# Moving the weighting with k–q products behind the substitution, in a two-layer hybrid encoder

## The chip, the cores and the metric

The kernel runs on one core of a Trainium2 chip. The metric is the device time of one execution in microseconds; the number compared is the median over several runs.

## The reference

The model has two residual layers over 256 tokens of 1024 channels. In each layer the normalised input is projected once into eleven segments. One branch is a bidirectional gated delta rule (8 heads, width 128), the other a differential softmax attention. Both are gated, projected, merged and projected out; a last RMSNorm closes. What the change touches is the delta rule:

```python
qkv = silu(short_conv(concat([q, k, v]), conv_w))     # 5 taps
q, k = l2norm(heads(q)), l2norm(heads(k))
decay = where(lower, exp(g_i - g_j), 0)                # g = cumulated log decays
L  = where(strict, (k*beta) @ k.T * decay, 0)
T  = inverse(eye + L)                                  # triangular solve
u, w = T @ (v*beta), T @ (k*beta*exp(g))
qk = where(lower, q @ k.T * decay, 0)
# per chunk: v_new = u - w @ state
#            o     = q*exp(g) @ state + qk @ v_new
#            state = state*exp(g_last) + (k*exp(g_last - g)).T @ v_new
```

It runs forwards and backwards, and the two outputs are added.

## The kernel before, in words

**Chunks and directions.** The kernel uses two chunks (`c`) of 128 tokens instead of the reference's 64, and keeps both directions (`d`) side by side. Heads are handled in two groups (`g`) of four.

**Projections.** Each is a stream over four pairs of weight rows (`kp`). A pair of 128 x 1024 elements is loaded (`raw`, L226, from SyncE's queue), cast to a high part (`hi`, L230, ScalarE) and reduced to a low part (`lo`, L232, VectorE: `raw − hi`). TensorE then does three matmuls per tile: hi with hi, lo with hi, hi with lo (L244–L246 token-major, L298–L302 feature-major). There are three buffers for `raw` and two each for `hi` and `lo`.

**Convolutions.** `conv` evacuates a feature-major projection of q, k or v: five taps on VectorE (L523 on ScalarE, L527 on VectorE), a tanh, a product, a transposition, and squares on ScalarE (L556). Group 1 of q (`conv("q", C_QA, 1, 1)`) is the last one ahead of the substitution.

**Decays.** `decays(g, c)` broadcasts the decay rows from DRAM into `B` (L618, issued from GpSimd's queue), lets GpSimd add to `kds` (L621) and mask (L624), and lets ScalarE take eight exponentials (L628). `weigh_k(g, c)` adds both directions (`dsum`, L634), forms the products of k with k on TensorE (`gram`, L611) and multiplies the two into `A` (L635). `weigh_q(g, c)` forms the products of k with q and multiplies them into `B` (L639, 128 x 1024 elements).

**Substitution.** `turn_blocks` exponentiates `kds` and stores the diagonal 32 x 32 blocks of `A` to DRAM and loads them back in another layout (L654–L657, GpSimd's queue). `take_blocks` copies them (L664), held behind the last q convolution. `substitute(0, 31)` does 62 VectorE operations (L670, L671), each depending on the one before it. `spread_blocks` copies and stores the result to `udr` (L674, L678).

**Merges and chunks.** `merges(g)` loads the blocks back (T64 at L705, U at L709) and joins them on TensorE (`y64p` at L723, `zt`, `z`, `y128p`, `zt128`). `chunks(g)` runs the recurrence; its second step scales k by the decays on GpSimd (L795, `ktm<-ktm,kds`, four products of 128 x 512 a layer) and its last step reads `B` (L821).

**Order.** A scheduler orders each engine's instructions by their place in the program and by a simulated time; attention heads (`head`), projections and the delta rule are interleaved in that way. `behind(ins)`, which is `tc.issue_after(ins)`, adds that what is traced in its block is queued behind `ins` on `ins`'s engine; `mark` holds such instructions. `bank_c` are two PSUM banks that the grams share with the convolutions' transpositions and the merges.

Of the kernel before, what the change touches and what calls it, by code (L numbers as in the profile page):

```python
# [12 lines left out]
ALU = mybir.AluOpType  # L13
# [4 lines left out]
P = 128  # L18
# [31 lines left out]
def hybrid_encoder(  # L50
# [47 lines left out]
    def last(ap, n):  # L98
        return ap.unsqueeze(ap.ndim).to_broadcast(list(ap.shape) + [n])
# [104 lines left out]
    def behind(ins):  # L204
        return nullcontext() if ins is None else tc.issue_after(ins)

    def weights(w, c0, n, nm, homes=(None,) * 4, ahead=True, later=None, spare=(), held=None):

        for kp in range(4):
            act, dve = (later or {}).get(kp, (None, None))
            with tc.high_priority(offset=HP) if ahead and homes[kp] is None else nullcontext():
                if homes[kp] is not None:
                    hi, lo = homes[kp][:, 0], homes[kp][:, 1]
                else:
                    hi = wpool.tile([P, 2, 512], F32R, tag="hi", name=f"hi_{nm}{kp}", bufs=2)
                    lo = wpool.tile([P, 2, 512], F32R, tag="lo", name=f"lo_{nm}{kp}", bufs=2)
                if kp in spare:  # L220
                    raw = work.tile([P, 2, 512], F32, tag="w4a", name=f"raw_{nm}{kp}", bufs=2)
                else:
                    raw = wpool.tile([P, 2, 512], F32, tag="raw", name=f"raw_{nm}{kp}", bufs=3)
                load = (held or {}).get(kp)
                with behind(load):
                    (nc.scalar if load else nc.sync).dma_start(  # L226
                        out=raw[:, :, :n],
                        in_=w[kp * 256 : (kp + 1) * 256, c0 : c0 + n].rearrange("(k p) c -> p k c", p=P))
                with behind(act):
                    high = S.copy(hi[:, :, :n], raw[:, :, :n]).ins  # L230
                with behind(dve):
                    mark[nm, kp] = high, V.tensor_tensor(lo[:, :, :n], raw[:, :, :n],  # L232
                                                         hi[:, :, :n].bitcast(F32), ALU.subtract).ins
            for k in range(2):
                yield 2 * kp + k, hi[:, k, :n], lo[:, k, :n]

    def proj_tm(act, w, c0, n, evac, nm, places=(None,) * 4, spare=(), later=None):

        accs = banks2(f"pp_{nm}")
        for kt, hi, lo in weights(w, c0, n, nm, places, later=later, spare=spare):  # L240
            for m in range(NM):
                ts_ = slice(m * P, (m + 1) * P)
                o = accs[m][:, :n]
                T.matmul(o, act[kt // 4][:, 0, kt % 4, ts_], hi, start=kt == 0, stop=False)  # L244
                T.matmul(o, act[kt // 4][:, 0, kt % 4, ts_], lo, start=False, stop=False)  # L245
                mark["proj"] = T.matmul(o, act[kt // 4][:, 1, kt % 4, ts_], hi, start=False,  # L246
                                        stop=kt == KT - 1).ins
                mark["done", kt] = mark["proj"]
        for m in range(NM):
            evac(m, accs[m][:, :n])  # L250
# [33 lines left out]
            evac(m, o)  # L284
            yield

    def proj_fm(act, w, c0, evac, nm):


        accs = [a.rearrange("p (b t) -> p b t", b=2) for a in banks2(f"pf_{nm}")]  # L290
        for kt, hi, lo in weights(w, c0, 512, nm, later=mark.pop("later", None)):
# [49 lines left out]
    for l in range(DEPTH):  # L341
# [98 lines left out]
        def qk_part(s_, i):  # L440
                def evac_qk(m, ps):
# [11 lines left out]
                    for b in range(4):  # L453
# [62 lines left out]
        def conv(seg, c_base, slot, g):  # L516
            def evac_conv(acc, b0):
# [86 lines left out]
        B = big.tile([P, NM, NH, 2, P], F32, tag="B", name=f"B{l}")  # L604
        kds = small.tile([P, 2, NH], F32, tag="kds", name=f"kds{l}")

        def gram(nm, g, c, slot):
            gp = bank_c(f"{nm}{l}{g}{c}")
            for j4 in range(4):
                kqh = kq[:, 4 * g + j4, c]  # L610
                T.matmul(gp[:, j4 * P : (j4 + 1) * P], kqh[:, 0, :], kqh[:, slot, :],  # L611
                         start=True, stop=True)
            return heads4(gp)

        def decays(g, c):
            hs4 = slice(4 * g, 4 * g + 4)
            dec = B[:, c, hs4].rearrange("p h d i -> p d h i")
            G.dma_start(out=B[:, c, hs4].rearrange("p h d i -> p (h d i)"),  # L618
                        in_=gdr[c, hs4].rearrange("h d i -> (h d i)").partition_broadcast(P))
            end = (P - 1) * (1 - c)  # L620
            G.tensor_tensor(kds[:, c, hs4], dec[:, c, :, end], lnc[:, c, c, hs4], ALU.add)  # L621
            for d in range(2):
                sg = 1 - 2 * d
                G.affine_select(out=dec[:, d], in_=dec[:, d], compare_op=ALU.is_ge, fill=BIG,  # L624
                                base=0, pattern=[[0, 4], [sg, P]], channel_multiplier=-sg)
                for j4 in range(4):
                    h = 4 * g + j4
                    S.activation(dec[:, d, j4, :], dec[:, d, j4, :], AF.Exp,  # L628
                                 bias=lnc[:, d, c, h : h + 1])

        def weigh_k(g, c):
            dec = B[:, c, 4 * g : 4 * g + 4].rearrange("p h d i -> p d h i")
# [1 line left out]
            V.tensor_tensor(dsum, dec[:, 0], dec[:, 1], ALU.add)  # L634
            V.tensor_tensor(A[:, g, c], gram("kk", g, c, 0), dsum, ALU.mult)  # L635

        def weigh_q(g, c):
            bv = B[:, c, 4 * g : 4 * g + 4]
            V.tensor_tensor(bv, gram("kq", g, c, 1).unsqueeze(2).to_broadcast([P, 4, 2, P]), bv, ALU.mult)  # L639


        osb = lambda g, c: kq[:, 4 * g : 4 * g + 4, c, 1, :]
# [28 lines left out]
                V.tensor_tensor(X[:, :nr, j + 1 :], X[:, :nr, j + 1 :], tv, ALU.subtract)  # L671

        def spread_blocks():
            V.tensor_copy(lt, X.rearrange("p c i -> p i c"))  # L674
            for d in range(2):
                ps_ = slice(64 * d, 64 * d + 64)
                for w, src_ in enumerate((X, lt) if d == 0 else (lt, X)):
                    G.dma_start(out=udr[w, :, :, 8 * d : 8 * d + 8].rearrange("b g t j i -> (b g) (t j i)"),  # L678
                                in_=src_[ps_].rearrange("p j i -> p (j i)"))


        tix = lambda d, c, j4: (2 * d + c) * 4 + j4
# [92 lines left out]
        def chunks(g):  # L775
# [16 lines left out]
                S.copy(flat(y1[d]), ps)  # L792
            yield
            for d in range(2):
                G.tensor_tensor(st[d], st[d], last(kds[:, d, hs4], P), ALU.mult)  # L795
# [282 lines left out]
```

## Time and profile before

| | |
|---|---|
| median of 3 runs | 779.93 us (778.48 to 781.05) |
| span of the profiled execution (first to last instruction) | 777.1 us |
| its launch time | not listed; the nearest figures are the runs above |
| TensorE (PE) busy | 758.2 us, 98% |
| VectorE (DVE) busy | 557.3 us, 72% |
| ScalarE (ACT) busy | 474.9 us, 61% |
| GpSimd (POOL) busy | 101.9 us, 13% |
| granted TensorE clock | 0.996 |

The engines run side by side, so the busy times add up to far more than the span. Matmuls are pipelined: two of them overlap in the trace, so a busy TensorE isn't necessarily at its peak. In lines of groups and waits, `a<-b` is what is written and what is read; `<-ENGINE tile Lnn` is what ended the idle time before.

### The profile page before, as it was taken

What the parts mean: (1) busy time and instruction counts of PE and PEld (TensorE: products, weight loads), DVE (VectorE), ACT (ScalarE), POOL (GpSimd) and SP (SyncE); (2) the same over time, 40 slices, a digit from 0 to 9 for tenths busy, and PEclk for the clock granted to TensorE, in tenths of its full rate; (3) what the DMA queues carried; (4) which work ended last, traced back from release to release, by engine and by line L of the source; (5) the groups of instructions that cost most, each with busy time, mean ns of one, the idle gap of its engine ahead of it and who ended that gap; (6) DMA issues with size and microseconds to landing.
All of it is one profiled execution on the core that took longest, in us unless ns stands there. A gap on an engine that the chain in (4) does not pass through costs nothing.

```text
span 777.1 us, 13805 instructions
## 1 busy us (share of the span) xinstructions
PE 758.2 (98%) x5222; PEld 647.7 (83%) x5222; DVE 557.3 (72%) x1051; ACT 474.9 (61%) x1042; POOL 101.9 (13%) x137
## 2 busy tenths in 40 slices
PE   8999999999999999999999999999999999999996
PEld 4899879887778888887889888899777788888784
DVE  5686878999974635377677776989999553536782
ACT  5657776557677744564554668655577776356551
POOL 5100461100030100010010025510001110001000
PEclk9999999999999999999999999999999999999998
DMA  7752756554496644346664256755446954343631
GB/s 227 240 177 78 224 146 198 174 172 136 112 207 187 210 135 129 117 144 210 215 224 136 82 160 221 194 170 161 141 137 174 233 164 160 114 133 111 213 110 54
DMA packets 77745, 126.91 MB, mean 163 GB/s; under 512 B 19679, under 2 KB 20015, under 8 KB 77680
## 3 DMA queue, kind: packets, MB, share of 16 engines
q1 hardware_dynamic: 71038, 112.99, 48.4%
q0 software_dynamic: 3936, 9.77, 4.8%
q10 hardware_dynamic: 2706, 3.28, 1.3%
q8 instruction: 41, 0.67, 0.4%
q14 instruction: 24, 0.20, 0.1%
HBM read 121.27 MB, written 4.75 MB: 162 GB/s over the span
## 4 chain that ended last, share of the span: by engine, by line
PE 81%; DVE 7%; DMA 5%; ACT 4%; issue 2%; POOL 0%; SPq 0%; POOLq 0%; ACTq 0%; DVEq 0%
PE pp_vb L282 5%; DMA raw_q<-in_w_in_dram 3%; PE pp_qk L245 2%; PE pp_qk L246 2%; PE pp_qk L244 2%; PE pp_o L282 2%; PE pf_k L298 2%; PE pf_k L302 2%; PE pf_v L298 2%; PE pf_k L300 2%; PE pp_gb L245 2%; PE sc L839 2%; PE pp_gb L244 2%; PE pf_v L302 2%; PE pf_v L300 2%; PE av L865 2%
## 5 line engine op out<-in xcount | busy, mean ns | idle before, releaser
L245 PE MATMUL pp_qk<-lo_qk,hT 128*128 128x512 f32 x128 | 51.3, 401 | 1.0 <-DVE lo_qk L232 1.0
L246 PE MATMUL pp_qk<-hi_qk,hT 128*128 128x512 f32 x128 | 50.1, 391 | 0.0
L230 ACT CAST hi_qk<-raw_qk 128x1024 fp32r<-128x1024 f32 x32 | 33.5, 1046 | 23.6 <-PE pp_qk L246 12.6
L244 PE MATMUL pp_qk<-hi_qk,hT 128*128 128x512 f32 x128 | 46.1, 398 | 0.7 <-ACT hi_qk L230 0.7
L232 DVE TENSOR_TENSOR lo_qk<-raw_qk,hi_qk 128x1024 fp32r<-128x1024 f32 x32 | 40.2, 1257 | 7.6 <-ACT hi_qk L230 7.4
L232 DVE TENSOR_TENSOR lo_pb<-raw_pb,hi_pb 128x1024 fp32r<-128x1024 f32 x16 | 19.6, 1224 | 35.7 <-ACT hi_pb L230 35.7
L298 PE MATMUL pf_q<-hT,hi_q 128*128 128x256 f32 x128 | 36.5, 288 | 0.3 <-ACT hi_q L230 0.2
L298 PE MATMUL pf_v<-hT,hi_v 128*128 128x256 f32 x128 | 36.5, 289 | 0.0
L300 PE MATMUL pf_v<-hT,hi_v 128*128 128x256 f32 x128 | 36.2, 286 | 0.0
L300 PE MATMUL pf_q<-hT,hi_q 128*128 128x256 f32 x128 | 35.9, 284 | 0.0
L848 ACT ACTIVATE es<-sc,mx 128x256 f32<-128x256 f32 x64 | 29.8, 473 | 10.1 <-DVE mx L846 10.0
L298 PE MATMUL pf_k<-hT,hi_k 128*128 128x256 f32 x128 | 35.8, 285 | 0.0
L302 PE MATMUL pf_q<-hT,lo_q 128*128 128x256 f32 x128 | 35.7, 292 | 0.0
L300 PE MATMUL pf_k<-hT,hi_k 128*128 128x256 f32 x128 | 35.7, 283 | 0.0
L232 DVE TENSOR_TENSOR lo_gb<-raw_gb,hi_gb 128x1024 fp32r<-128x1024 f32 x16 | 19.6, 1224 | 22.2 <-ACT hi_gb L230 22.0
L232 DVE TENSOR_TENSOR lo_ga<-raw_ga,hi_ga 128x1024 fp32r<-128x1024 f32 x16 | 19.6, 1226 | 21.0 <-ACT hi_ga L230 21.0
L302 PE MATMUL pf_v<-hT,lo_v 128*128 128x256 f32 x128 | 34.6, 286 | 0.0
L302 PE MATMUL pf_k<-hT,lo_k 128*128 128x256 f32 x128 | 34.4, 285 | 0.0
L230 ACT CAST hi_pb<-raw_pb 128x1024 fp32r<-128x1024 f32 x16 | 16.8, 1049 | 25.1 <-PE pp_pb L246 24.3
L527 DVE SCALAR_TENSOR_TENSOR cvq<-pf_q,cw,cvq 128x254 f32<-128x254 f32 (+1 forms) x64 | 29.7, 476 | 1.8 <-ACT cvq L523 1.4
L527 DVE SCALAR_TENSOR_TENSOR cvv<-pf_v,cw,cvv 128x254 f32<-128x254 f32 (+1 forms) x64 | 30.2, 483 | 0.6 <-ACT cvv L523 0.5
L527 DVE SCALAR_TENSOR_TENSOR cvk<-pf_k,cw,cvk 128x254 f32<-128x254 f32 (+1 forms) x64 | 28.5, 478 | 2.0 <-ACT cvk L523 1.3
(356 smaller groups left out, 2495.5 us busy)
## 6 DMA issues: line engine op xcount, KB each, us to landing
raw_qk<-in_w_in_dram SPq DMA_DIRECT2D x32, 512.0 KB, 3.7
raw_k<-in_w_in_dram SPq DMA_DIRECT2D x16, 512.0 KB, 4.6
raw_q<-in_w_in_dram SPq DMA_DIRECT2D x16, 512.0 KB, 3.7
raw_v<-in_w_in_dram SPq DMA_DIRECT2D x16, 512.0 KB, 3.8
raw_zb<-in_w_in_dram SPq DMA_DIRECT2D x16, 512.0 KB, 3.6
raw_za<-in_w_in_dram SPq DMA_DIRECT2D x16, 512.0 KB, 3.7
raw_gb<-in_w_in_dram SPq DMA_DIRECT2D x16, 512.0 KB, 4.7
raw_o<-in_w_out_dram SPq DMA_DIRECT2D x16, 512.0 KB, 4.5
```

Source lines behind the costliest of these rows:

```text
L230: high = S.copy(hi[:, :, :n], raw[:, :, :n]).ins
L232: mark[nm, kp] = high, V.tensor_tensor(lo[:, :, :n], raw[:, :, :n], hi[:, :, :n].bitcast(F32), ALU.subtract).ins
L244: T.matmul(o, act[kt // 4][:, 0, kt % 4, ts_], hi, start=kt == 0, stop=False)
L245: T.matmul(o, act[kt // 4][:, 0, kt % 4, ts_], lo, start=False, stop=False)
L246: mark["proj"] = T.matmul(o, act[kt // 4][:, 1, kt % 4, ts_], hi, start=False, stop=kt == KT - 1).ins
L282: mark["proj"] = T.matmul(o, a_, w_, start=kt == 0 and a_ is ah and w_ is hi, stop=kt == KT - 1 and a_ is al).ins
L298: T.matmul(o, hi[:, cs], act[kt // 4][:, 0, kt % 4, :], start=first, stop=False, skip_group_check=True)
L300: T.matmul(o, hi[:, cs], act[kt // 4][:, 1, kt % 4, :], start=False, stop=False, skip_group_check=True)
L302: T.matmul(o, lo[:, cs], act[kt // 4][:, 0, kt % 4, :], start=False, stop=done, skip_group_check=True)
L527: V.scalar_tensor_tensor(ca[:, o0:o1], acc[:, b, o0 + sft : o1 + sft], cw[:, j, cb : cb + 1], ca[:, o0:o1], ALU.mult, ALU.add)
L839: mm = T.matmul(sp[n][:, qt * SEQ : (qt + 1) * SEQ], qkT[h // 4][rows, 0, h % 4, qt * P : (qt + 1) * P], qkT[h // 4][rows, 1, h % 4, :], s ...
L848: S.activation(es[:, n, qt, :], spv[:, qt, :], AF.Exp, bias=mx[:, n, qt : qt + 1], accum_out=s_all[:, h, n, qt : qt + 1])
```

## The change

Four things are changed.

1. The four calls of `weigh_q` move from around the last q convolution, ahead of the substitution, to a place behind `head(5)`. Each gram is held behind a matmul of the projection traced last before it there (the first half of za, rows 1, 3, 5 and 7).
2. Three casts of weights a layer go from ScalarE to VectorE: the last pair of q's group 1, and the first two pairs of the second half of the attention's k.
3. The broadcasts of the decays of group 1 are traced behind the exponentials of the first decays.
4. GpSimd's four products with k are queued behind the last store to `udr`.

```diff
-                    high = S.copy(hi[:, :, :n], raw[:, :, :n]).ins
+                    high = (V.tensor_copy if kp in turned else S.copy)(hi[:, :, :n], raw[:, :, :n]).ins
...
-                proj_tm(hT, wl, (C_QB, C_KB)[s_] + 512 * i, 512, evac_qk, f"qk{l}{s_}{i}")
+                proj_tm(hT, wl, (C_QB, C_KB)[s_] + 512 * i, 512, evac_qk, f"qk{l}{s_}{i}",
+                        turned=(0, 1) if (s_, i) == (0, 1) else ())
...
-            proj_fm(hT, wl, c_base + 512 * g, evac_conv, f"{seg}{l}{g}")
+            proj_fm(hT, wl, c_base + 512 * g, evac_conv, f"{seg}{l}{g}",
+                    turned=(3,) if (seg, g) == ("q", 1) else ())
...
-        def gram(nm, g, c, slot):
+        def gram(nm, g, c, slot, after=None):
...
-                T.matmul(gp[:, j4 * P : (j4 + 1) * P], kqh[:, 0, :], kqh[:, slot, :],
-                         start=True, stop=True)
+                with behind(after):
+                    T.matmul(gp[:, j4 * P : (j4 + 1) * P], kqh[:, 0, :], kqh[:, slot, :],
+                             start=True, stop=True)
...
-        def decays(g, c):
+        def decays(g, c, after=None):
...
-            G.dma_start(out=B[:, c, hs4].rearrange("p h d i -> p (h d i)"),
-                        in_=gdr[c, hs4].rearrange("h d i -> (h d i)").partition_broadcast(P))
+            with behind(after):
+                G.dma_start(out=B[:, c, hs4].rearrange("p h d i -> p (h d i)"),
+                            in_=gdr[c, hs4].rearrange("h d i -> (h d i)").partition_broadcast(P))
...
-                    S.activation(dec[:, d, j4, :], dec[:, d, j4, :], AF.Exp,
-                                 bias=lnc[:, d, c, h : h + 1])
+                    mark["decay", d] = S.activation(dec[:, d, j4, :], dec[:, d, j4, :], AF.Exp,
+                                                    bias=lnc[:, d, c, h : h + 1]).ins
...
-        def weigh_q(g, c):
+        def weigh_q(g, c, after):
...
-                    G.dma_start(out=udr[w, :, :, 8 * d : 8 * d + 8].rearrange("b g t j i -> (b g) (t j i)"),
-                                in_=src_[ps_].rearrange("p j i -> p (j i)"))
+                    mark["udr"] = G.dma_start(out=udr[w, :, :, 8 * d : 8 * d + 8].rearrange("b g t j i -> (b g) (t j i)"),
+                                in_=src_[ps_].rearrange("p j i -> p (j i)")).ins
...
-                G.tensor_tensor(st[d], st[d], last(kds[:, d, hs4], P), ALU.mult)
+                with behind(mark["udr"]):
+                    G.tensor_tensor(st[d], st[d], last(kds[:, d, hs4], P), ALU.mult)
...
         weigh_k(0, 0)
+        seen = mark["decay", 0], mark["decay", 1]
         decays(0, 1)
         weigh_k(0, 1)
-        decays(1, 0)
+        decays(1, 0, seen[0])
         weigh_k(1, 0)
-        decays(1, 1)
+        decays(1, 1, seen[1])
         weigh_k(1, 1)
         turn_blocks()
-        weigh_q(0, 0)
-        weigh_q(0, 1)
         conv("q", C_QA, 1, 1)
         take_blocks()
         qk_part(0, 1)
-        weigh_q(1, 0)
-        weigh_q(1, 1)
         substitute(0, 31)
...
         head(5)
+        for g in range(2):
+            for c in range(NM):
+                weigh_q(g, c, mark["done", 4 * g + 2 * c + 1])
         z_part(za, C_ZA, "za", 1)
```

More of the change, by code (lines that the diff above doesn't have):

```diff
@@ L205, in behind, with weights @@
         return nullcontext() if ins is None else tc.issue_after(ins)
-    def weights(w, c0, n, nm, homes=(None,) * 4, ahead=True, later=None, spare=(), held=None):
+    def weights(w, c0, n, nm, homes=(None,) * 4, ahead=True, later=None, spare=(), held=None, turned=()):
         for kp in range(4):
@@ L235, in weights, with proj_tm @@
                 yield 2 * kp + k, hi[:, k, :n], lo[:, k, :n]
-    def proj_tm(act, w, c0, n, evac, nm, places=(None,) * 4, spare=(), later=None):
+    def proj_tm(act, w, c0, n, evac, nm, places=(None,) * 4, spare=(), later=None, turned=()):
         accs = banks2(f"pp_{nm}")
-        for kt, hi, lo in weights(w, c0, n, nm, places, later=later, spare=spare):
+        for kt, hi, lo in weights(w, c0, n, nm, places, later=later, spare=spare, turned=turned):
             for m in range(NM):
@@ L285, in proj_by_tile, with proj_fm @@
             yield
-    def proj_fm(act, w, c0, evac, nm):
+    def proj_fm(act, w, c0, evac, nm, turned=()):
         accs = [a.rearrange("p (b t) -> p b t", b=2) for a in banks2(f"pf_{nm}")]
-        for kt, hi, lo in weights(w, c0, 512, nm, later=mark.pop("later", None)):
+        for kt, hi, lo in weights(w, c0, 512, nm, later=mark.pop("later", None), turned=turned):
             for b in range(4):
@@ L635, in weigh_k @@
             V.tensor_tensor(A[:, g, c], gram("kk", g, c, 0), dsum, ALU.mult)
-        def weigh_q(g, c):
+        def weigh_q(g, c, after):
             bv = B[:, c, 4 * g : 4 * g + 4]
-            V.tensor_tensor(bv, gram("kq", g, c, 1).unsqueeze(2).to_broadcast([P, 4, 2, P]), bv, ALU.mult)
+            V.tensor_tensor(bv, gram("kq", g, c, 1, after).unsqueeze(2).to_broadcast([P, 4, 2, P]), bv, ALU.mult)
         osb = lambda g, c: kq[:, 4 * g : 4 * g + 4, c, 1, :]
@@ L673, in spread_blocks @@
         def spread_blocks():
-            V.tensor_copy(lt, X.rearrange("p c i -> p i c"))
+            mark["spread"] = V.tensor_copy(lt, X.rearrange("p c i -> p i c")).ins
             for d in range(2):
```

## The prediction

> **What bounds the kernel now.** I read the page's busy times first, then the table of waits for TensorE alone, then sums by stage around the changed code, and last the timelines of the engines at the two places where work leaves and arrives.
>
> ```profile
> span 777.1 us, 13805 instructions
> ## 1 busy us (share of the span) xinstructions
> PE 758.2 (98%) x5222; PEld 647.7 (83%) x5222; DVE 557.3 (72%) x1051; ACT 474.9 (61%) x1042; POOL 101.9 (13%) x137
> ```
>
> TensorE is busy for 98% of the span, and the change takes no matmul away. So the only thing to win is its idle time: 777.1 − 758.2 = 18.9 us, part of it at the two ends. The waits of TensorE in the whole span (total, times, longest; a wait listed twice occurs once in each layer):
>
> ```profile
> PE wb_n L145 <- POOL tri L113: 3.1, 1, 3.1
> PE kk L611 <- DVE A L635: 1.3, 2, 0.8
> PE pp_pa L245 <- DVE lo_pa L232: 1.1, 2, 0.5
> PE pp_qk L245 <- DVE lo_qk L232: 1.0, 2, 0.5
> PE pp_zb L244 <- ACT es L848: 0.9, 2, 0.5
> PE pp_qk L244 <- ACT hi_qk L230: 0.7, 2, 0.5
> ...
> PE pf_q L298 <- ACT hi_q L230: 0.2, 1, 0.2
> ```
>
> Four of these (kk, lo_qk, hi_qk, hi_q) belong to the code that is changed, 1.3 + 1.0 + 0.7 + 0.2 = 3.2 us in both layers. The stages show where they lie (length, then busy us of PE, PEld, DVE, ACT, POOL):
>
> ```profile
> 95.00:112.00 17.00, 15.23 (x109) 13.56 (x108) 10.78 (x14) 15.43 (x46) 12.04 (x14) 1.00 0.51 174
> 112.00:137.00 25.00, 25.00 (x173) 23.15 (x172) 22.39 (x40) 13.64 (x30) 5.52 (x9) 1.00 0.71 199
> 137.00:172.00 35.00, 35.00 (x214) 30.59 (x213) 34.08 (x79) 19.57 (x36) 3.20 (x1) 1.00 0.56 167
> 172.00:216.00 44.00, 43.55 (x225) 34.00 (x225) 42.93 (x102) 30.69 (x78) 0.00 (x0) 1.00 0.45 132
> 216.00:233.00 17.00, 17.00 (x100) 13.31 (x100) 12.09 (x20) 13.42 (x39) 6.18 (x12) 1.00 1.02 208
> 473.00:490.00 17.00, 15.45 (x111) 13.81 (x110) 10.97 (x15) 15.34 (x46) 12.18 (x15) 1.00 0.52 179
> ```
>
> From 95 to 112 us TensorE is idle for 1.77 us, and for 1.55 us at the same place of layer 1 (473 to 490); ScalarE is the loaded engine there. From 137 to 216 VectorE is full with the substitution, yet TensorE loses only 0.45 us: that stretch is not where time can be won. An idle gap costs a little more than it shows, because a matmul that follows another starts before that one is done:
>
> ```profile
> 87.12 0.39 PE L244 MATMUL pp_qk<-hi_qk,hT 128*128 128x512 f32 x1
> 87.34 0.39 PE L245 MATMUL pp_qk<-lo_qk,hT 128*128 128x512 f32 x1
> ```
>
> They start 0.22 us apart and take 0.39, so each gap hides about 0.17 us more. With seven gaps the two stages hold 3.2 + 7 × 0.17 = 4.4 us. That is the ceiling of what the aimed-at stalls can give.
>
> **The change part by part.** *Casts on VectorE.* Why ScalarE is late:
>
> ```profile
> 98.61 1.05 ACT L230 CAST hi_q<-raw_q 128x1024 fp32r<-128x1024 f32 x1 [1.20 <-DMA raw_q<-in_w_in_dram]
> ...
> 101.53 3.61 ACT L628 ACTIVATE B<-B,lnc 128x128 f32<-128x128 f32 x12
> 105.04 1.03 ACT L230 CAST hi_qk<-raw_qk 128x1024 fp32r<-128x1024 f32 x1
> ```
>
> The cast of the last q weights waits 1.20 us for its load and takes 1.05, and the remaining exponentials of the decays stand behind it. Taken off ScalarE, it lets them run 2.25 us earlier. The sums and products behind them (dsum, then A) come earlier by as much, more than the longest kk wait of 0.8 us: I count 1.3 us gone. The first cast of the k weights (L230 hi_qk) stands behind twelve exponentials; off that queue its 0.7 us of waits go. The cast of the last q weights needs the same late load on any engine, so the 0.2 us stays.
>
> What VectorE must pay: no copy of this kind is in the trace. The nearest rows are the transposing copy of the same size and ScalarE's cast above.
>
> ```profile
> L674 DVE COPY lt<-X x2: 1101/1111/1121, 216.2 to 594.5; 128x1024 f32<-128x1024 f32 x2
> ```
>
> ```profile
> L634 DVE TENSOR_TENSOR dsum<-B x8: 691/693/968, 97.5 to 487.0; 128x512 f32<-128x512 f32 x8
> L639 DVE TENSOR_TENSOR B<-kq,B x8: 1217/1221/1225, 112.4 to 521.3; 128x1024 f32<-128x1024 f32 x8
> ```
>
> Bounds per cast: 0.69 (an operation on half the elements, L634) to 1.22 us (L639). I take 1.11, the copy of the same size: 3.33 us a layer. Is there room? VectorE is busy 10.78 of 17 us. Following its order from the landing near 98.6: cast 1.11, low part 1.22, dsum and A 1.38, cast 1.11, low part 1.22 are 6.04 us, so the first low part of k is there at 104.6. Before, it came at 108.39 (row below, 106.63 + 1.76); TensorE, freed of its 1.6 us of waits a layer and four refills (0.7), would ask for it near 106.1. The next block (dsum, A, cast, low part) takes 3.71 us, to 108.3, while TensorE needs 12 matmuls, 2.7 us, to 108.8: nearly level. For that I charge 0.3 us a layer (between 0 and 1.1, one whole cast).
>
> [...]
>
> *GpSimd's products with k.* Four a layer leave this place:
>
> ```profile
> 106.27 6.45 POOL L795 TENSOR_TENSOR ktm<-ktm,kds 128x512 f32<-128x512 f32 x4 [4.09 <-ACT kds L651]
> 112.67 0.73 POOL L654 DMA_DIRECT2D adr<-A  x1
> ```
>
> ```profile
> 106.63 1.76 DVE L232 TENSOR_TENSOR lo_qk<-raw_qk,hi_qk 128x1024 fp32r<-128x1024 f32 x1
> ...
> 113.57 1.22 DVE L232 TENSOR_TENSOR lo_qk<-raw_qk,hi_qk 128x1024 fp32r<-128x1024 f32 x1
> ```
>
> The low part beside these products took 1.76 us, a later one 1.22: 0.54 longer, and TensorE waited 0.5 for just that one in each layer. Both 0.5 go, 1.0 us. The stores of A (adr) stand behind the products and can go some 2 us earlier; that gives nothing, because the copy that consumes them is held behind the last q convolution. Where the products land:
>
> ```profile
> 216.71 1.25 POOL L678 DMA_DIRECT2D udr<-X  x2 [72.29 <-DVE X L671]
> 217.95 1.10 POOL L678 DMA_DIRECT2D udr<-lt  x2
> 221.67 0.31 POOL L701 MEMSET T<- 32x256 f32 x1 [2.62 <-DMA udr<-X]
> 222.03 0.31 POOL L702 MEMSET T<- 32x256 f32 x1
> 224.67 2.62 POOL L705 DMA_DIRECT2D T<-udr  x4 [2.33 <-DMA udr<-lt]
> ```
>
> ```profile
> T<-udr POOLq DMA_DIRECT2D x8, 64.0 KB, 4.1
> ```
>
> ```profile
> 232.93 0.31 PE L723 MATMUL y64p<-T,A 32*32 32x32 f32 x10
> ```
>
> Placed directly after the stores, they run from 219.05 to 225.5 and the two memsets to 226.1: the loads of T leave 1.4 us later than at 224.67. They land now about 224.67 + 2.62 + 4.1 = 231.4, 1.5 us ahead of their first reader at 232.93. So I cost this at nothing; that cover is thin.
>
> *Weighting with the products of k and q.* The grams are the same matmuls, so no TensorE time. Four multiplications of 1.22 us (L639), 4.88 us, leave VectorE between 112 and 145, two of them inside the full stretch, and return after 205, where VectorE is busy 12.09 of 17 us from 216 to 233. The full stretch can thus end some 2.4 us earlier or more. For TensorE that removes at most the es wait near 177: 0.9 us in both layers plus two refills, 1.2; half of it, 0.6, is my term (0 to 1.2).
>
> *Decay broadcasts.* They are traced under an order behind a ScalarE instruction, but the broadcast is issued from GpSimd's queue. The helper (issue_after) ties only instructions of the named instruction's own engine, so I expect this guard to hold nothing back: 0.
>
> **Sum**: waits 1.3 + 0.7 + 1.0 = 3.0, six refills 1.0, es 0.6, less 2 × 0.3 for VectorE: −4.0 us. The profiled execution has a span of 777.1; its own launch time is not listed, and the three runs (778.48 to 781.05) lie 1.4 to 4.0 above that span. On the median: 779.93 − 4.0 = **775.9**; span 773.1.
>
> **The rivals.** *The broadcasts do move* (0.10). Two of four broadcasts would then leave the path of the late q load.
>
> ```profile
> B<-gdr POOLq DMA_DIRECT2D x8, 512.0 KB, 8.7
> ```
>
> The load's 1.20 us of wait would go, and with it the last 0.2, its refill and the VectorE charge, 1.0 together: 774.9. Against it: the last two decays would land some 8.7 us after the first exponentials, near 105, and could push A out again.
>
> *VectorE's queue stalls instead* (0.20). A cast that waits for its load now holds VectorE. If it is put ahead of the first dsum at 97.50, then dsum, A and the q convolution queue behind it, and kk on TensorE behind A: 1.20 + 1.11 = 2.3 us a layer, 4.6 in all, against 4.0 won: 780.5 in full, 778.2 with half of it. For it: raw_q already ended an idle of ScalarE here. Against: the order on VectorE is planned around loads.
>
> *The merging starts late* (0.17, the slower side). y64p stands in TensorE's order in front of za, av and the next head, so its wait stops everything. If the weighting is put ahead of the last substitution steps, its move gives nothing back, and the casts (3.33 us) push the substitution's end that much; with the products 1.4 us in front of the T loads and 1.5 spare, and VectorE's work beside the products slowed there by 0.54 as L232 was, y64p waits 3.33 + 1.4 + 0.54 − 1.5 = 3.8 us a layer, 7.6 − 4.0 = +3.6: 783.5, more if part of the gain fails too. It decides from T loads issued later than about 226.2.
>
> **How the numbers follow.** Forecast 0.53, broadcasts 0.10, VectorE's queue 0.20, merging 0.17. A measurement here tells apart about 0.3%, 2.3 us: faster is below 777.6, slower above 782.3. Faster: 0.46 + 0.09 + 0.04 = 0.59; same: 0.07 + 0.01 + 0.14 + 0.02 = 0.24; slower: 0 + 0 + 0.02 + 0.15 = 0.17. The forecast's own range is 774.3 (4.4 and 1.2 in full) to 778.1 (a whole cast charged in each layer, no es term). For 8 in 10: 773.0, below both gaining cases by the scatter of the runs, to 782.0, which takes in the VectorE case and the milder half of the last.
>
> **What would show it.** Right: in the waits of TensorE the rows kk, lo_qk and hi_qk gone or below half, TensorE over 16.3 of 17 us busy at 95 to 112, lo_qk at 1.22, the casts near 1.1, and VectorE's last substitution step before 214. The broadcasts still leave together near 87. Wrong: a new TensorE wait on a cast or on A at the same place, or y64p waiting for T. A faster kernel without the waits of 95 to 112 shrinking would refute the reason, not the number.

## The result, and the profile after

| kernel | median us | lowest to highest | ratio to before, 95% interval |
|---|---|---|---|
| before | 779.09 | 778.08 to 781.05 | 1 |
| after | 776.33 | 774.41 to 779.15 | 0.9964 [0.9954, 0.9974] |

The change makes the kernel faster by 0.36%, 2.8 us, where 4.0 had been predicted. It lies inside the range on record (773.0 to 782.0).

The profiled execution of the changed kernel took 779.15 us, the longest of all of its runs and about the median of before. Its span (777.3) and its busy times therefore show no gain over before (777.1); the waits and the stages can be read. From the store of gdr of layer 0 to that of layer 1 it took 461.44 − 85.02 = 376.4 us, before 462.03 − 83.65 = 378.4: 2.0 us less. From there to the end it took 0.8 us more than before, and up to the first store 1.4 us more.

The page's first lines, and the waits of TensorE (total, times, longest), as far as they answer to the rows of before:

```profile
span 777.3 us, 13803 instructions
## 1 busy us (share of the span) xinstructions
PE 758.6 (98%) x5222; PEld 649.4 (84%) x5222; DVE 562.4 (72%) x1057; ACT 470.8 (61%) x1036; POOL 98.8 (13%) x137
```

```profile
PE wb_n L145 <- POOL tri L113: 3.1, 1, 3.1
PE pf_q L298 <- DVE hi_q L230: 1.8, 1, 1.8
...
PE pf_q L302 <- DVE lo_q L232: 0.6, 1, 0.6
...
PE ctq L545 <- DVE kq L537: 0.3, 1, 0.3
PE pp_zb L244 <- ACT es L853: 0.3, 2, 0.2
```

The rows kk (1.3), lo_qk (1.0) and hi_qk (0.7) are gone. New is a wait of TensorE for the last q weights: 1.8 + 0.6 + 0.3, where 0.2 stood. The same two stages as before:

```profile
95.00:112.00 17.00, 16.06 (x113) 14.49 (x113) 13.51 (x20) 13.32 (x48) 7.40 (x12) 1.00 0.65 217
...
473.00:490.00 17.00, 15.03 (x98) 13.79 (x97) 11.67 (x16) 12.74 (x45) 5.75 (x10) 0.90 0.54 175
```

TensorE is idle for 0.94 us in the first of these stages (before 1.77) and for 1.97 in the second (before 1.55). So in this execution the new wait takes back most of what the old ones gave. In layer 1 the granted clock, third from the end of a line, falls as well: it is 0.50 for 3.4 us from 479.2, from the end of TensorE's gap on. One microsecond of it:

```profile
480.00:481.00 1.00, 0.85 (x4) 0.58 (x3) 1.00 (x2) 0.73 (x4) 1.00 (x2) 0.50 0.07 27
```

Matmuls of 128 x 256 start 0.21 to 0.22 us apart there and 0.11 to 0.12 behind it, so 3.4 us hold 1.7 us less work of TensorE, by an estimate. The profile of before shows such a stretch only at its very end, from 771 us. VectorE's timeline, in layer 0 and then in layer 1:

```profile
99.77 0.91 DVE L230 CAST hi_q<-raw_q 128x1024 fp32r<-128x1024 f32 x1 [3.21 <-DMA raw_q<-in_w_in_dram]
100.78 1.23 DVE L232 TENSOR_TENSOR lo_q<-raw_q,hi_q 128x1024 fp32r<-128x1024 f32 x1
101.92 1.12 DVE L638 TENSOR_TENSOR dsum<-B 128x512 f32<-128x512 f32 x1
...
104.34 0.68 DVE L230 CAST hi_qk<-raw_qk 128x1024 fp32r<-128x1024 f32 x1
104.94 0.68 DVE L638 TENSOR_TENSOR dsum<-B 128x512 f32<-128x512 f32 x1
105.54 1.21 DVE L232 TENSOR_TENSOR lo_qk<-raw_qk,hi_qk 128x1024 fp32r<-128x1024 f32 x1
```

```profile
478.08 0.95 DVE L230 CAST hi_q<-raw_q 128x1024 fp32r<-128x1024 f32 x1 [5.10 <-DMA raw_q<-in_w_in_dram]
```

VectorE stands for 3.21 us, and for 5.10 in layer 1, before the cast of the last q weights: the cast is at the head of its queue and the load is not there. That load needs 10.4 and 12.3 us from issue to landing, where the median of the q loads is 3.7 (the longest before: 10.7). Four broadcasts are in flight with it; that they delay it is shown by `x_bcast` below:

```profile
88.07 2.18 POOL L622 DMA_DIRECT2D B<-gdr  x4 [1.83 <-ACT E L599]
```

The four still leave together: the new order of the broadcasts, behind a ScalarE instruction, has no effect. The products with k landed elsewhere than expected, between the two pairs of stores to udr. Their guard names the store that is traced last, and that is one of X, which leaves before those of the copy lt:

```profile
207.31 1.24 POOL L682 DMA_DIRECT2D udr<-X  x2 [69.03 <-DVE X L675]
208.57 5.31 POOL L800 TENSOR_TENSOR ktm<-ktm,kds 128x512 f32<-128x512 f32 x4
213.83 1.16 POOL L682 DMA_DIRECT2D udr<-lt  x2
...
217.84 2.61 POOL L709 DMA_DIRECT2D T<-udr  x4 [2.17 <-DMA udr<-lt]
```

The stores of X leave at 207.31 instead of 216.71, so the substitution ends 9.4 us earlier, and the loads of T leave at 217.84 instead of 224.67. Their first reader, y64p, starts at 232.7 (before 232.9), when TensorE gets to it: the waits list none of it for T, neither before nor now, so the lead of the loads wins nothing.

### The profile page after: what moved, and what is told of

The parts are those of the page before. It is cut to its first block, busy times and chain, and to the rows that moved or that the text cites. A ratio compares the mean times of both kernels' runs of the same rounds, so it can differ in the third digit from the quotient of the medians.

```text
span 777.3 us, 13803 instructions
## 1 busy us (share of the span) xinstructions
PE 758.6 (98%) x5222; PEld 649.4 (84%) x5222; DVE 562.4 (72%) x1057; ACT 470.8 (61%) x1036; POOL 98.8 (13%) x137
## 4 chain that ended last, share of the span: by engine, by line
PE 79%; DVE 10%; DMA 5%; ACT 3%; issue 2%; POOL 0%; SPq 0%; POOLq 0%; DVEq 0%; ACTq 0%
PE pp_vb L282 5%; PE pp_qk L244 2%; PE sc L844 2%; PE pp_qk L245 2%; PE pp_o L282 2%; DMA raw_vb<-in_w_in_dram 2%; PE pp_qk L246 2%; PE av L870 2%; PE pp_za L245 2%; PE pp_gb L245 2%; PE pp_gb L244 2%; PE pp_za L246 2%; PE pp_pb L246 2%; PE pp_pb L245 2%; PE pp_ga L246 2%
## 5 line engine op out<-in xcount | busy, mean ns | idle before, releaser
L232 DVE TENSOR_TENSOR lo_pb<-raw_pb,hi_pb 128x1024 fp32r<-128x1024 f32 x16 | 19.6, 1224 | 35.7 <-ACT hi_pb L230 35.7
L230 ACT CAST hi_qk<-raw_qk 128x1024 fp32r<-128x1024 f32 x28 | 29.4, 1051 | 26.1 <-PE pp_qk L246 15.5
L232 DVE TENSOR_TENSOR lo_qk<-raw_qk,hi_qk 128x1024 fp32r<-128x1024 f32 x32 | 39.1, 1221 | 6.0 <-ACT hi_qk L230 5.7
L232 DVE TENSOR_TENSOR lo_gb<-raw_gb,hi_gb 128x1024 fp32r<-128x1024 f32 x16 | 19.6, 1224 | 21.5 <-ACT hi_gb L230 21.3
L232 DVE TENSOR_TENSOR lo_ga<-raw_ga,hi_ga 128x1024 fp32r<-128x1024 f32 x16 | 19.6, 1225 | 21.0 <-ACT hi_ga L230 21.0
```

The source lines that it names most:

```text
L230: high = (V.tensor_copy if kp in turned else S.copy)(hi[:, :, :n], raw[:, :, :n]).ins
```

## The experiments

The theory from this profile: the waits of 95 to 112 are gone for the reason given, and the late q load under VectorE takes back about half. The rivals: one of the moved parts does the work alone, or one costs more than it gives. The parts are three (weighting, casts, products); the broadcasts' new order does nothing as written. All eight combinations were timed, before and after among them. One thing limits what a single cell says. The scheduler plans anew for each kernel, and in most cells several hundred of TensorE's 5222 matmuls stand elsewhere in its order (about a thousand between before and after). Where two kernels have the same order of TensorE and of VectorE, this is said.

**Products back** (`u_products`). TensorE's and VectorE's orders are those of the changed kernel; only GpSimd's order and a few load issues differ.

```diff
-                with behind(mark["udr"]):
+                with behind(None):
                     G.tensor_tensor(st[d], st[d], last(kds[:, d, hs4], P), ALU.mult)
```

> The kernel after, with GpSimd's four products a layer put back to their old place (ahead of the stores of A); only GpSimd's order differs. Theory A (the products slow VectorE's low parts beside them, and TensorE waits for those): lo_qk at 1.7 to 1.8 us again instead of 1.21, a lo_qk wait of about 0.5 us on TensorE in each layer again, time up by about 1.3 us against the kernel after: ratio to the kernel before 0.998. Theory B (the casts taken off ScalarE already made room enough): VectorE is slowed, but TensorE does not wait, ratio 0.9964 as after. Theory C (what counts is that the stores of A leave earlier): no difference on TensorE at 95 to 112 us, but a later substitution.

Measured: 781.33 us, 1.0041 [1.0025, 1.0058], 6.0 us more than the changed kernel by the ratios, where Theory A had 1.3. So this part, which the prediction counted at 1.0 us of wait and a refill or two, decides the sign: without it the rest of the change is slower than before. VectorE and then GpSimd at the old place, and TensorE's wait:

```profile
102.61 1.42 DVE L230 CAST hi_qk<-raw_qk 128x1024 fp32r<-128x1024 f32 x1
103.95 1.52 DVE L638 TENSOR_TENSOR dsum<-B 128x512 f32<-128x512 f32 x1
105.40 2.05 DVE L232 TENSOR_TENSOR lo_qk<-raw_qk,hi_qk 128x1024 fp32r<-128x1024 f32 x1
```

```profile
102.44 5.91 POOL L800 TENSOR_TENSOR ktm<-ktm,kds 128x512 f32<-128x512 f32 x4 [0.63 <-ACT kds L655]
```

```profile
PE pp_qk L245 <- DVE lo_qk L232: 4.1, 2, 2.3
```

The casts free ScalarE, so kds is ready earlier: the products start at 102.44 instead of 106.27 and now lie beside three operations that the next matmuls need. Each of the three is 0.7 to 0.85 us longer than the same line in the changed kernel (1.42 against 0.68, 1.52 against 0.68, 2.05 against 1.21). In layer 1 the wait, 1.8 us, lies in a stage (473 to 490) with a mean granted clock of 0.94; the stage of layer 0 (95 to 112) has 1.00.

**Weighting back** (`u_weigh`), the four calls ahead of the substitution again:

```diff
         turn_blocks()
+        weigh_q(0, 0, None)
+        weigh_q(0, 1, None)
         conv("q", C_QA, 1, 1)
...
         qk_part(0, 1)
+        weigh_q(1, 0, None)
+        weigh_q(1, 1, None)
...
-        for g in range(2):
-            for c in range(NM):
-                weigh_q(g, c, mark["done", 4 * g + 2 * c + 1])
```

> The kernel after, with the weighting by the products of k and q back ahead of the substitution. Theory A (the gain comes from the stage of the decays, from casts and GpSimd's products): waits of TensorE at 95 to 112 us stay as after, only the wait for es behind the stretch full of VectorE work returns (0.9 instead of 0.3 us): ratio 0.997. Theory B (the gain comes from emptying VectorE ahead of and during the substitution): the whole gain is gone, ratio 0.999 to 1.002.

Measured: 783.36 us, 1.0064 [1.005, 1.0078]. Again slower than before. VectorE, GpSimd and the wait:

```profile
214.56 5.32 DVE L232 TENSOR_TENSOR lo_za<-raw_za,hi_za 128x1024 fp32r<-128x1024 f32 x1
```

```profile
214.76 4.03 POOL L800 TENSOR_TENSOR ktm<-ktm,kds 128x512 f32<-128x512 f32 x4
```

```profile
PE pp_za L245 <- DVE lo_za L232: 3.7, 2, 1.9
...
PE pp_za L244 <- DVE za L313: 1.4, 2, 0.7
```

The substitution ends later, so the products land beside a low part of za, which takes 5.32 us instead of 1.22 (1.22 + 4.03 = 5.25): it stands until the fourth product is done. In the changed kernel a low part of za, started 0.96 us after the first product, took 1.45.

**One part alone** (`only_weigh`, `only_casts`, `only_products`) **and casts back** (`u_casts`). `u_casts` sets `turned=()` in both calls; `only_weigh` does that and `behind(None)`; `only_casts` does `behind(None)` and puts the weighting back; `only_products` sets `turned=()` and puts the weighting back.

```diff
-                        turned=(0, 1) if (s_, i) == (0, 1) else ())
+                        turned=())
...
-                    turned=(3,) if (seg, g) == ("q", 1) else ())
+                    turned=())
```

> The kernel before with the weighting moved alone (casts on ScalarE, GpSimd's products in the old place). Theory A (the three parts hold each other: the weighting alone only empties VectorE where TensorE did not wait): kk, lo_qk and hi_qk waits as before, es wait 0.3 instead of 0.9, ratio 0.999 to 1.001. Theory B (each part gives its own term): ratio 0.9985 for the es term alone; or, if the weighting is the whole gain, 0.996.

> The kernel before with the three casts on VectorE alone. Theory A (freed exponentials let the products with k start earlier, next to the casts and low parts that TensorE now waits for, and VectorE is slowed for as long as they run): lo_qk waits of about 2 us a layer, ratio 1.003 to 1.006, as when the products were put back. Theory B (each part its own term, as the prediction summed them: 2.0 us of waits and 0.7 of refills, less 0.6): ratio 0.997.

> The kernel before with GpSimd's products behind the stores of the substitution alone. Theory A (they land beside a low part of za on VectorE, which stood still for 4.1 us beside them when the weighting alone was put back): lo_qk waits at 108 us gone (1.0 us), lo_za waits of about 1.9 us a layer new, ratio 1.002 to 1.006. Theory B (own term, 1.3 us won, nothing lost): ratio 0.998.

> The kernel after with the three casts back on ScalarE (weighting and products moved). Theory A (the casts on VectorE remove the waits for hi_qk and kk and were worth about 2 us net): waits for hi_qk and for kk return, ratio 0.998 to 0.999. Theory B (what the casts win the late load of q on VectorE's queue takes back): ratio 0.996 as after.

Measured (the eight cells; us is the ratio less 1, times 779):

| weighting | casts | products | kernel | ratio, 95% interval | us |
|---|---|---|---|---|---|
| – | – | – | before | 1 | 0 |
| moved | – | – | only_weigh | 1.0002 [0.999, 1.0013] | +0.2 |
| – | moved | – | only_casts | 1.0054 [1.0039, 1.007] | +4.2 |
| – | – | moved | only_products | 1.0085 [1.0068, 1.0102] | +6.6 |
| moved | moved | – | u_products | 1.0041 [1.0025, 1.0058] | +3.2 |
| – | moved | moved | u_weigh | 1.0064 [1.005, 1.0078] | +5.0 |
| moved | – | moved | u_casts | 1.0051 [1.0034, 1.0067] | +4.0 |
| moved | moved | moved | after | 0.9964 [0.9954, 0.9974] | −2.8 |

No part alone gains; two of them alone are slower; every pair is slower; all three are faster. The single effects add up to +11.0 us, the whole is −2.8. A sum over parts can't describe this. The ratios expected for `u_products`, `u_weigh` and `u_casts` were all missed, and `only_products` lost more than its Theory A said, on another operation. What the five losing cells have in common is seen where the products run. `only_casts`, GpSimd, and VectorE beside it:

```profile
104.07 5.95 POOL L800 TENSOR_TENSOR ktm<-ktm,kds 128x512 f32<-128x512 f32 x4 [1.30 <-ACT kds L655]
```

```profile
105.62 2.06 DVE L232 TENSOR_TENSOR lo_qk<-raw_qk,hi_qk 128x1024 fp32r<-128x1024 f32 x1
```

`only_products`, GpSimd, VectorE (the first of the two takes 4.87 us by itself, its usual time is 0.48) and TensorE's wait:

```profile
217.70 4.04 POOL L800 TENSOR_TENSOR ktm<-ktm,kds 128x512 f32<-128x512 f32 x4
```

```profile
217.16 5.27 DVE L861 SCALAR_TENSOR_TENSOR es<-es,cc 128x256 f32<-128x256 f32 x2
```

```profile
PE at L864 <- DVE es L861: 3.9, 3, 1.5
```

`u_casts`, VectorE, the first product there at 211.82:

```profile
211.62 5.33 DVE L232 TENSOR_TENSOR lo_za<-raw_za,hi_za 128x1024 fp32r<-128x1024 f32 x1
```

In each, the four products meet an operation on which TensorE waits next: lo_qk, the scaling of the attention (es) or lo_za. What another part moves is only *where* they meet. Casts back, for instance, lets the stores of X leave at 210.55 instead of 207.31, and the products fall on lo_za. Two pairs of the table have the same order of TensorE and of VectorE and differ in the products' place alone: `u_products` and the changed kernel (6.0 us), `only_weigh` and `u_casts` (3.8 us). `only_weigh` leaves products and casts as before and comes out even; its waits of TensorE show kk as before, a new one on es, and the one of pp_zb:

```profile
PE at L864 <- DVE es L861: 2.7, 2, 1.4
...
PE kk L614 <- DVE A L639: 1.3, 2, 0.8
PE pp_zb L244 <- ACT es L853: 1.0, 2, 0.5
```

The wait of pp_zb is the one that the prediction gave to the weighting. It stays at 1.0 here and in `u_casts`, and at 0.9 where the casts move without the weighting (`only_casts`); it is 0.3 only where both have moved.

**The collision by itself** (`only_products_late`, `u_weigh_late`). If it is the meeting that costs, and not the products' absence from the old place or the delay of the T loads, then the same products put behind the last memset of the T blocks, some 9 to 10 us later, should cost nothing. The edit, made to `only_products` and to `u_weigh`:

```diff
-            G.memset(T64[blk(3), 8:16, 0:32], 0.0)
+            mark["t64"] = G.memset(T64[blk(3), 8:16, 0:32], 0.0).ins
...
-                with behind(mark["udr"]):
+                with behind(mark["t64"]):
```

> The kernel before with GpSimd's products moved alone, to behind the last memset of the T blocks. Theory A (the collision, not the move, cost 6.6 us when they were put directly behind the stores): no VectorE operation of 5 us unless one is met there too, lo_qk wait at 108 us gone, ratio from 1.0085 down to 0.997 to 1.000. Theory B (the late products hold up the stores and loads or the recurrence): ratio stays above 1.004.

> Weighting in the old place, casts on VectorE, GpSimd's products still later: behind the last memset of the merges' T blocks instead of directly behind the first stores of the substitution. VectorE's order is that of the kernel with the weighting put back. Theory A (products back to back hold any VectorE operation with two SBUF inputs until they end; in that kernel lo_za stood for 5.3 us and TensorE behind it): lo_za at 1.22 us again unless the products meet another such operation, its waits of 1.9 us a layer gone, ratio from 1.0064 down to 0.996 to 1.000. Theory B (the weighting ahead of the substitution is itself the cost, because the merges come late): ratio stays at 1.005 or more.

Measured: `only_products_late` 778.83 us, 0.9996 [0.9984, 1.0007] (1.0085 before the edit: 6.9 us); `u_weigh_late` 777.77 us, 0.9982 [0.9969, 0.9994] (1.0064: 6.4 us). In `only_products_late`, GpSimd, then VectorE beside it, then a wait that stayed:

```profile
227.57 6.00 POOL L800 TENSOR_TENSOR ktm<-ktm,kds 128x512 f32<-128x512 f32 x4
```

```profile
227.76 3.90 DVE L232 TENSOR_TENSOR lo_za<-raw_za,hi_za 128x1024 fp32r<-128x1024 f32 x2 [1.44 <-ACT hi_za L230]
```

```profile
PE kk L614 <- DVE A L639: 0.9, 2, 0.5
```

They still meet lo_za, but the two low parts take 3.90 instead of some 2.4 us and TensorE has no wait for them. So the meeting costs 6.4 to 6.9 us where VectorE stands the whole time, and nothing here. In the first pair, `only_products`, part of that can be TensorE's order, which differs in about 500 matmuls; in `u_weigh` it differs only at the first matmuls of y64p and the za beside them. Part is the granted clock: the four runs of `only_products` have a mean of 0.993 to 0.996 against 0.996 to 0.998. Two more pairs share the orders of TensorE and VectorE: `only_casts` and `u_weigh_late` differ by 5.6 us, before and `only_products_late` by 0.3.

The products' move as such is worth nothing measurable (0.9996): the lo_qk waits go, and the 1.0 us that the prediction counted for them is not in the time. Its profile has new waits of TensorE instead, 0.8 us for hi_q where 0.2 stood and 0.8 in front of z. With the products out of the way the other parts can be estimated: `u_weigh_late` gives the casts 0.9982 − 0.9996, about 1.1 us, and the weighting on top of them 0.9964 − 0.9982, about 1.4 us. Both differences contain a new order of TensorE, and the second also the products' way from the memsets back to the stores. The intervals touch or overlap, so the sizes are rough; the sign of both together, −2.5 us, is clear (0.9964 against 0.9996).

**The late load** (`u_qcast`, `x_bcast`). First the q cast alone back to ScalarE; second the broadcasts really moved, by a guard on an instruction of GpSimd, from whose queue they are issued.

```diff
-                    turned=(3,) if (seg, g) == ("q", 1) else ())
+                    turned=())
```

```diff
-                G.affine_select(out=dec[:, d], in_=dec[:, d], compare_op=ALU.is_ge, fill=BIG,
-                                base=0, pattern=[[0, 4], [sg, P]], channel_multiplier=-sg)
+                mark["mask", d] = G.affine_select(out=dec[:, d], in_=dec[:, d], compare_op=ALU.is_ge, fill=BIG,
+                                                  base=0, pattern=[[0, 4], [sg, P]], channel_multiplier=-sg).ins
...
-        seen = mark["decay", 0], mark["decay", 1]
+        seen = mark["mask", 0], mark["mask", 1]
```

> The kernel after, with the cast of the last q weights back on ScalarE (the two k casts stay on VectorE). Theory A (taking it off ScalarE freed the exponentials behind it): kk waits on TensorE come back with about 0.6 us a layer, time up by 1 to 2 us against the kernel after, ratio 0.998. Theory B (on VectorE it holds dsum, A and the convolution behind a late load, and that cost what the profile of after shows in layer 1, a wait of 1.8 us for hi_q): time down by 0.5 to 1.5 us, ratio 0.995.

> The kernel after, with the broadcasts of group 1's decays really held back: behind GpSimd's two masks of the first decays, on GpSimd's own queue. Theory A (four broadcasts in flight delay the last load of q, and the cast on VectorE waits for it): the load lands 3 to 4 us after issue-plus-two-broadcasts, near 95 instead of 99.7 us, the waits of TensorE for hi_q and lo_q (1.8 and 0.6 in the profile of after) go, and the ratio falls to 0.993 to 0.995. Theory B (the later decays make A late instead): waits of TensorE for A or kk of 1 us a layer, ratio 0.998 to 1.001.

Measured: `u_qcast` 773.15 us, 0.9932 [0.992, 0.9944]; `x_bcast` 772.79 us, 0.9921 [0.9909, 0.9933]. Both beat the changed kernel, by 2.5 and 3.3 us by the ratios, with an order of TensorE that is the changed kernel's but for a few dozen matmuls at most, around the last q weights. In `u_qcast` the first stage is full, by the busy times of the stages, and one wait for hi_q remains, in layer 1, on ScalarE now:

```profile
95.00:112.00 17.00, 17.00 (x123) 15.67 (x121) 13.71 (x21) 15.03 (x47) 7.02 (x11) 1.00 0.64 218
```

```profile
PE pf_q L298 <- ACT hi_q L230: 1.4, 1, 1.4
```

In `x_bcast` the broadcasts leave two, one, one (GpSimd's timeline); VectorE doesn't stand before the cast (its timeline); both stages are full (busy times):

```profile
87.19 1.14 POOL L622 DMA_DIRECT2D B<-gdr  x2 [1.83 <-ACT E L599]
...
93.41 0.58 POOL L622 DMA_DIRECT2D B<-gdr  x1
...
95.66 0.55 POOL L622 DMA_DIRECT2D B<-gdr  x1
```

```profile
96.26 0.73 DVE L230 CAST hi_q<-raw_q 128x1024 fp32r<-128x1024 f32 x1
```

```profile
95.00:112.00 17.00, 17.00 (x121) 15.66 (x120) 16.27 (x21) 13.77 (x45) 8.35 (x11) 1.00 0.60 194
...
473.00:490.00 17.00, 17.00 (x111) 15.47 (x110) 16.37 (x24) 12.28 (x41) 4.68 (x7) 1.00 0.63 195
```

The load lands 7.8 us after its issue at 88.3 instead of 10.4; in layer 1 the cast starts at 471.9 instead of 478.08, without a wait for the load. So two different cures of the same wait, another queue for the cast or an earlier landing, each return what the prediction had left out.

**Both cures, and the products later too** (`x_bcast_q`: `x_bcast` with the q cast on ScalarE; `x_bcast_late`: `x_bcast` with the products behind the memsets). The edits are those shown above.

> The kernel after with group 1's broadcasts really held back, and the cast of the last q weights back on ScalarE. Theory A (the q cast on VectorE hurts only through the late load; with the load early it relieves ScalarE): ratio 0.993 to 0.996, worse than 0.9921 with the cast on VectorE. Theory B (the q cast on VectorE is a loss in itself): ratio 0.991 or less, both gains together.

> The kernel after with group 1's broadcasts really held back and GpSimd's products behind the last memset of the T blocks. Orders of TensorE, VectorE and ScalarE are those of the kernel with the broadcasts held back. Theory A: there the products already fall beside operations that read PSUM, so little is left to win, ratio 0.991 to 0.993; if they now meet a low part, 0.994 to 0.997. Theory B (the products in front of the second half of the stores delay the merges): ratio 0.989 or less.

Measured: `x_bcast_late` 772.72 us, 0.9915 [0.9898, 0.9931], a tie with `x_bcast`: there the four products take 5.31 us as in the changed kernel, where the low part beside them takes 1.45, and a later place brings nothing. `x_bcast_q` 789.49 us, 1.0136 [1.0113, 1.0159], outside what either theory expected. Its waits of TensorE:

```profile
PE sc L844 <- ACT es L853: 4.5, 3, 2.1
PE at L864 <- DVE es L861: 3.7, 2, 1.9
```

The scheduler, which plans by simulated times, wrote another order for TensorE too, and the products again fell on es (205.82 to 209.85, es 4.87 us long). The run thus says nothing on the q cast. Part of its loss is the granted clock: 0.88 from 233 to 262, a stage in which TensorE is idle for 2.1 us (1.00 and none in `x_bcast`), and 0.991 over the profiled execution against 0.997, some 5 us of TensorE's work by an estimate. Its six runs have a mean clock of 0.985 to 0.991, those of `x_bcast` 0.997 to 0.998. Why the new order waits 4.5 us on sc was not settled.

## Why the prediction was right, and where not

**Casts: mechanism right.** kk, lo_qk and hi_qk, 3.0 us of waits, are gone, as said. The casts of k took 0.68 us and those of q 0.91 and 0.95, not the 1.11 taken from the transposing copy; that was the wrong row. The lower bound given beside it, 0.69 from dsum, was the nearer. The 4.4 us given as the ceiling of these stalls, 5.6 with the es term in full, were not the limit: `x_bcast` gained 6.2. In its profile TensorE is idle for 14.9 us instead of 18.9 and busy for 1.8 less; where that lies was not followed up.

**The charge for VectorE, the mis-sized term.** The step "the cast of the last q weights needs the same late load on any engine, so the 0.2 us stays", with 0.3 us a layer charged, failed. On ScalarE the late load held up exponentials (the cast waited 1.20 us, before); at the head of VectorE's queue it holds up VectorE for 3.21 and 5.10 us, and TensorE then waits for the cast and what stands behind it. Casting q on ScalarE returns 2.5 us (`u_qcast`), where 0.6 was charged. A new wait of TensorE on a cast is what the prediction itself had named as a sign of being wrong; it came, 1.8 us in layer 1. The cast went ahead of the first dsum, 97.50 before and 101.92 now, just as the second rival said; its price of 4.6 was too high: TensorE had no wait for A behind it. TensorE, expected busy for over 16.3 of 17 us at 95 to 112, was busy for 16.06; the missing 0.94 are the waits for lo_q (0.6) and in front of ctq (0.3) behind that cast. −4.0 + (2.5 − 0.6) = −2.1, close to the measured −2.8; other terms were off as well (below), so the closeness is partly luck. The granted clock is in no term.

**The weighting: right in the sum, not as a part of its own.** The es wait of pp_zb fell from 0.9 to 0.3, the 0.6 of the term, and the substitution ended before 214 (206.7). But moved alone it left that wait at 1.0 and won nothing (`only_weigh`): the wait goes only with the casts. About 1.4 us is estimated for it beside the casts, a little over its 0 to 1.2, with TensorE's new order in it.

**The products: wrong as a term.** They were given 1.0 us and "costed at nothing" at the new place, with the T loads as the danger. They were expected behind all four stores, but their guard let them go behind those of X. The loads of T came 6.8 us earlier instead of later, and the move alone is worth nothing. What the step lacked was the question whom the products run beside at the landing place, though the prediction had its row: lo_qk took 1.76 instead of 1.22 beside them. That 0.54 was a mild meeting; a low part can be held for 4.1. In the changed kernel they happen to land beside one low part, which takes 1.45, and else mostly beside operations that read PSUM, which keep their 0.68 and 1.21 us:

```profile
210.91 0.68 DVE L851 TENSOR_REDUCE mx<-sc 128x2 f32<-128x512 f32 x1
211.51 1.21 DVE L643 TENSOR_TENSOR B<-kq,B 128x1024 f32<-128x1024 f32 x1
```

That L643 is a weighting operation that was moved: the parts fit together, which a sum over parts could not see. That the total came out near was therefore partly luck of places.

**The broadcasts: right.** They leave together at 88.07, and a guard on GpSimd's own instruction does move them. The rival priced that at 1.0 us; it is 3.3, since it contains the mis-sized charge.

**The third rival** (late merging) did not happen: T's loads issue at 217.84, far from the 226.2 at which it decides.

**What stayed open.** Why an operation of VectorE is sometimes held for 4.1 us by the products and sometimes for 0.85 (below); how much of the gain belongs to the moved parts and how much to TensorE's new order; what makes the granted clock fall; the size of the q cast's effect under moved broadcasts.

## What to carry to other kernels

Price a moved operation by what runs beside it where it lands, and not only by what it leaves: four products of 4.03 us held a low part for 4.1 in `u_weigh`. Parts that move one another's landing place have to be tried in combination, since here each pair loses (3.2 to 5.0 us) and the three together win (2.8). Where a scheduler plans anew for every edit, read a part from kernels whose other orders are the same. A cast that waits for a load took its wait along to VectorE's queue here (3.21 and 5.10 us), so ask who stands behind such an operation there. An order guard on an instruction of ScalarE left GpSimd's four broadcasts together at 88.07, one on an instruction of GpSimd moved two of them to 93.41 and 95.66; check in the trace that a guard did something. Beside a new wait of TensorE, read the granted clock behind it (0.50 for 3.4 us in the changed kernel).

## What the runs showed of the hardware

**GpSimd and VectorE hold each other.** Beside GpSimd's products of two SBUF operands, VectorE's operations on two SBUF operands take longer (L232 1.22 us alone, 1.45 in the changed kernel, up to 5.33 in `u_casts`; dsum 0.68 and 1.52 in `u_products`; es 0.48 and 4.87 in `only_products`), and so does the cast (0.68 and 1.42 in `u_products`). Reductions and products that read PSUM keep their time (mx 0.68, L643 1.21 in the changed kernel). The products are lengthened as well: in `x_bcast_late` a low part of za starts 0.23 us before the first product and keeps its time, and that product takes 1.89 us, where those of `u_weigh` take 1.03 to 1.05.

```profile
216.16 1.23 DVE L232 TENSOR_TENSOR lo_za<-raw_za,hi_za 128x1024 fp32r<-128x1024 f32 x1 [0.45 <-ACT hi_za L230]
```

```profile
216.39 1.89 POOL L800 TENSOR_TENSOR ktm<-ktm,kds 128x512 f32<-128x512 f32 x1
```

In the long cases the same lead goes with the opposite outcome: lo_za of `u_weigh` starts at 214.56, 0.20 us before the first product at 214.76, and yet stands through all four products, which run in 4.03, their shortest time. Since `x_bcast_late` has the same lead and a short case, the lead alone doesn't make a case long. What the long cases share, and `x_bcast_late` lacks, is that VectorE's operation starts while GpSimd is still issuing the stores of X (213.48 to 214.74 in `u_weigh`). That alone isn't enough either: in the changed kernel a low part starts at 207.78, within the stores of 207.31 to 208.55 and 0.8 us ahead of the first product, and takes 1.23. No run varies the two apart. In the short cases in which VectorE's operation starts after the first product, both are lengthened: low parts, dsum and the cast take 0.23 to 0.85 us more than alone, and the four products 4.4 us (`u_weigh_late`) to 6.45 (before) instead of 4.03.

**The granted clock.** In the profile of the changed kernel the clock granted to TensorE is 1.00 or 0.50. Once TensorE runs, and short of the end, it is 0.50 in one stretch, of 3.4 us, behind a wait of 1.8 us. In `u_products` the stage 473 to 490, with a wait of 1.8 us, has a mean of 0.94; in `x_bcast_q` the stage 233 to 262, with 2.1 us of idle time, has 0.88. Not every such wait goes with a lower clock: the mean is 1.00 in the stages 95 to 112 and 112 to 137 of `u_products`, with a wait of 2.3 us in layer 0, and in 216 to 233 of `u_weigh`, with one of about 1.9. What decides was not tested.

**Contention of loads.** In the changed kernel a load of 128 x 1024 weights, 512 KB, beside four broadcasts of 512 KB took 10.4 and 12.3 us to land. In `x_bcast`, with two of them ahead of it and a third issued 5 us into it, it took 7.8 in layer 0. The median of the changed kernel's sixteen q loads is 3.7.
